# Second key stack of one stick-breaking head computed from its PSUM bank by ACT and DVE instead of two transfers from POOL's queue

## The chip, the cores and the metric

The kernel runs on one core of one Trainium2 chip. The metric is the device time of one execution in microseconds, given as the median of several runs. The engines are TensorE (PE, the matmuls), VectorE (DVE), ScalarE (ACT), GpSimd (POOL) and SyncE (SP); SP, ACT and POOL issue transfers on queues of their own. All data are float32.

## What is computed

The reference is two transformer blocks over 512 tokens of width 1024. The change lies in the first block's attention, which has four differential heads and eight stick-breaking heads of 64 dimensions. A stick-breaking head computes, in blocks of 128 queries:

```python
z = jnp.einsum('bhqd,bhkd->bhqk', q_blk, k).astype(jnp.float32) * scale
log_beta = jax.nn.log_sigmoid(z)
log_1mb = jnp.where(strict, jax.nn.log_sigmoid(-z), 0.0)
between = lax.cumsum(log_1mb, axis=3, reverse=True) - log_1mb
a = jnp.where(strict, jnp.exp(log_beta + between), 0.0)
return jnp.einsum('bhqk,bhkd->bhqd', a.astype(v.dtype), v)
```

A differential head takes two softmax maps p0 and p1 (with a position bias) and applies p0 - lam * p1 to its values; lam comes from four vectors of 64 numbers. The rest of the program is the projections, the gated feed-forward parts and the second block's mixer.

## The kernel before

Matmul operands are split into a rounded high part and the rest (`whi` by ACT's copy L107, `wlo` by a subtraction on DVE or POOL, L108), and a product is three matmuls (L128 to L130). A projection writes a PSUM bank; there are eight banks, and `PLAN_1` gives each kind of tile its banks by number.

Queries and keys come two heads to a bank, 64 partitions each. `stack_q` makes for each head one tile `qs` with the high part in 64 partitions and the rest in the other 64. `stack_k` makes `ka`, which holds the high part at the head's own partitions and the rest at the others, and `kb`, which is `ka` with its two halves exchanged. `ka` is computed from the bank: a copy on ACT (L417) and a subtraction on DVE (L418). `kb` is filled by two transfers from SBUF to SBUF on POOL's queue (L419 and L420), 64x512 numbers or 128 KB each. A score block is then two matmuls, `ka` by `qs` and `kb` by `qs` (L442), which add up all four products of the parts.

`start()` makes the stacks of the first pair of heads, S0 and S1, from banks 0 (`ps_mm_238`, queries) and 2 (`ps_s_239`, keys), and those of the second pair. Head `r` of a pair is the first (0) or the second (1). Then come, in the order of `PLAN_1`: the tables of the position bias (two gathers `rev` from the DRAM tile `scratch`, on POOL's queue, L382) and lambda (four loads into `lv`, L391 to L396), the first value projection v0 (banks `ps_mm_492` and `ps_mm_493`, `natural`), the heads S0 to S3, the second value projection v1 (`ps_mm_985` and `ps_mm_984`) and further projections, S4 to S7, and the differential heads D0 to D3.

A stick-breaking head has three units of scores, one bank each (S0: `ps_n_607`, `622`, `636`; S1: `700`, `715`, `729`). The steps of a unit: scores L442 and a mask L445; Abs, Exp and Ln on ACT (L448 to L450); maximum and sum on DVE (L451); the split `sph` and `spl` (L454 and L455); the cumulative sums on PE (L460 to L470); Exp on ACT into `a` (L476); the split `ah` and `al` (L481 and L482); the values on PE (L485 and L486). L678 and L679 add the two halves of its output `ot`. Value projections are evicted by L588 (ACT) and L589 (DVE). A differential head has scores L518, logits L508 (DVE), Exp L538 (ACT), lambda's factor L540 and L541, the difference of the maps on DVE (L547) or POOL (L544 and L545), transposes L568, evictions L121 and L122, and values L554.

The order on each engine is set by a scheduler at build time, with a cost model of its own, after the program has been recorded in `PLAN_1`'s order. So a change of one operation moves others.

Of the kernel before, what the change touches and what calls it, by code (L numbers as in the profile page):

```python
# [37 lines left out]
def f32(ap):  # L38
    return ap.bitcast(F32)
# [360 lines left out]
def stack_q(cx, q, r, pool, scale, t=None):  # L400

    nc = cx.nc
    a, b = slice(64 * r, 64 * r + 64), slice(64 - 64 * r, 128 - 64 * r)
    if t is None:
        t = pool.tile([P, T], F32R, tag="q", bufs=cx.nq, name="qs")
    nc.scalar.activation(t[a], q[a], AF.Copy, scale=scale)
    nc.vector.scalar_tensor_tensor(t[b], q[a], scale, f32(t[a]), op0=ALU.mult, op1=ALU.subtract)
    return t


def stack_k(cx, q, r, pool):

    nc = cx.nc
    a, b = slice(64 * r, 64 * r + 64), slice(64 - 64 * r, 128 - 64 * r)
    u = pool.tile([P, T], F32R, tag="k", bufs=cx.nk, name="ka")
    v = pool.tile([P, T], F32R, tag="k", bufs=cx.nk, name="kb")
    nc.scalar.copy(u[a], q[a])  # L417
    nc.vector.tensor_sub(u[b], q[a], f32(u[a]))  # L418
    nc.gpsimd.dma_start(v[0:64], u[64:128])  # L419
    nc.gpsimd.dma_start(v[64:128], u[0:64])  # L420
    return u, v
# [188 lines left out]
def attention_1(cx, I, first, finish):  # L610

    nc, tc = cx.nc, cx.tc
    w = I["w_qkv"][0]
    with tc.tile_pool(name="att1", bufs=1, reuse_waits="tile") as pool:
# [13 lines left out]
            mix[k] = m  # L628
        Q, K, v, o, z = {}, {}, {}, {}, {}

        def stacks(n, q, k):

            for out, st, bank in ((Q, lambda b, r: stack_q(cx, b, r, pool, 0.125), q), (K, lambda b, r: stack_k(cx, b, r, pool), k)):
                if bank is not None:
                    out.setdefault(n, []).extend(st(bank, r) for r in range(2))

        def start():

            first.append(cx.fetch(w, 0, KD, [(1536 + P, P)]))
            ww = [cx.split(st, lo_on=e) for st, e in zip(first, (nc.gpsimd, nc.gpsimd, None))]  # L640
            banks = [cx.bank(i) for i in ("mm", "s", "mm")]
            for c in (slice(0, 256), slice(256, T)):
                for q, wi in zip(banks, ww):
                    cx.columns_of(q, wi, c, c.start == 0)
            stacks("s0", banks[0], None)
            stacks("s0", None, banks[1])
            stacks("s1", banks[2], None)
            stacks("s1", None, cx.columns(cx.split(cx.fetch(w, 0, KD, [(2048 + P, P)]))))

# [44 lines left out]
        for x in PLAN_1:  # L694
            if isinstance(x, dict):
                cx.share(**x)
            elif x[0] == "+":
                cx.lo_on = nc.gpsimd if x[1] == "p" else nc.vector
            elif x == "start":
                start()  # L700
            elif x == "tables":
                z["band"], z["lam"] = diff_tables(cx, I, pool)
            elif x[0] == "b":
                z[x] = z["band"](int(x[1]))
            elif x[0] == "S":
                sb(int(x[1]))
            elif x[0] == "D":
                diff(int(x[1]))
            elif x[0] == "n":
                norm(x[1:])  # L710
            elif x[0] in "vw":
                value(x)
            else:
                project(x)
# [281 lines left out]
def mixer(cx, I, finish):  # L996
# [4 lines left out]
    with tc.tile_pool(name="mixer", bufs=1, reuse_waits="tile") as pool:  # L1001
# [15 lines left out]
        def keys(c0):  # L1017
            st = cx.fetch(w, 0, KD, [(c0, 128)])
            q = cx.columns(cx.split(st))
            return [stack_k(cx, q, g, pool) for g in range(2)]  # L1020
# [14 lines left out]
        for c in (slice(0, 256), slice(256, T)):  # L1035
            for q, wi in zip(banks, ww):
                cx.columns_of(q, wi, c, c.start == 0)
        KB = [stack_k(cx, banks[0], g, pool) for g in range(2)]
        QB = [stack_q(cx, banks[1 + h // 2], h % 2, pool, scale(h)) for h in range(4)]
        cx.share(mm=(0, 1), s=(2, 3), t=(4, 5), o=(6, 7))  # L1040
# [335 lines left out]
```

## Time and profile before

| | us |
|---|---|
| median of 3 runs | 1645.98 (1645.66 to 1646.47) |
| the profiled execution | 1645.26 |
| its span, first to last instruction | 1643.5 |
| outside the span | 1.76 |
| PE busy | 1613.6 (98% of the span) |
| DVE, ACT, POOL busy | 844.3, 680.3, 212.3 |
| mean granted clock of TensorE | 0.997 |

The profiled execution is one run of its own; it lies 0.72 us below the median. The span is what the trace covers, and the 1.76 us beside it are the start and the end of the program. Busy shares are means over the whole span; the first block's attention lies in the first 262 us or so of it. All waits below are read from that one execution.

### The profile page before, as it was taken

Reading aid. Unit: us, or ns where it says so; the run is one execution under the profiler, and the core shown is the slowest. Engines: PE = TensorE matmul, PEld = TensorE weight load, DVE = VectorE, ACT = ScalarE, POOL = GpSimd, SP = SyncE. Lnnn points to the kernel's source line nnn. Section 1 sums busy time; section 2 is a strip of 40 time slices with the busy share of each in tenths; the row PEclk is TensorE's granted clock in tenths of the full one; section 3 lists DMA queues with packets and bytes.
Section 4 is the critical chain, followed back from the end, with each engine's and each line's share of the span. In section 5 each row is a group of like instructions: output and inputs, shape, how many; then the busy total and the mean of one; then the engine's idle time right before and its main releaser. Section 6 shows DMA issues by size and latency. Waiting matters only on the chain.

```text
span 1643.5 us, 21090 instructions
## 1 busy us (share of the span) xinstructions
PE 1613.6 (98%) x8354; PEld 1375.0 (84%) x8354; DVE 844.3 (51%) x1391; ACT 680.3 (41%) x1212; POOL 212.3 (13%) x291
## 2 busy tenths in 40 slices
PE   8999999999999999999999999999999999999998
PEld 7988987888888888888888888888878988888886
DVE  5667776666665235433333225687985533333232
ACT  4656565444444123323232223576874432222222
POOL 3044241000000001000000000034770000000000
PEclk9999999999999999999999999999999999999999
DMA  6434315433223234333332325462005532232231
GB/s 187 111 104 114 91 40 188 147 103 103 94 86 103 90 102 154 128 103 102 103 103 92 101 90 162 115 168 65 15 27 183 188 103 96 84 101 104 90 103 64
DMA packets 149451, 177.02 MB, mean 108 GB/s; under 512 B 5999, under 2 KB 116031, under 8 KB 149352
## 3 DMA queue, kind: packets, MB, share of 16 engines
q1 hardware_dynamic: 141798, 158.35, 29.9%
q0 software_dynamic: 4672, 7.87, 2.1%
q10 hardware_dynamic: 2882, 9.44, 1.5%
q8 instruction: 66, 1.08, 0.3%
q14 instruction: 33, 0.27, 0.1%
HBM read 159.37 MB, written 10.51 MB: 103 GB/s over the span
## 4 chain that ended last, share of the span: by engine, by line
PE 91%; DVE 3%; DMA 2%; ACT 2%; POOL 1%; issue 1%; SPq 0%; POOLq 0%; DVEq 0%; ACTq 0%
PE ps_mm L128 11%; PE ps_mm L129 11%; PE ps_mm L130 11%; PE ps_n L130 9%; PE ps_n L129 9%; PE ps_n L128 9%; PE ps_s L130 8%; PE ps_s L128 8%; PE ps_s L129 8%; PE ps_s L518 1%; PE ps_t L568 1%; PE ps_o L1086 1%; PE ps_o L1087 1%; PE ps_n L194 1%; DMA kb<-ka 1%
## 5 line engine op out<-in xcount | busy, mean ns | idle before, releaser
L108 DVE TENSOR_TENSOR wlo<-stage,whi 128x1024 fp32r<-128x1024 f32 (+1 forms) x242 | 297.7, 1232 | 462.8 <-ACT whi L107 459.1
L107 ACT CAST whi<-stage 128x1024 fp32r<-128x1024 f32 x256 | 268.2, 1050 | 604.1 <-PE ps_mm L129 200.6
L128 PE MATMUL ps_mm<-HT,whi 128*128 128x512 f32 (+1 forms) x824 | 306.7, 372 | 3.3 <-ACT HT L196 2.1
L129 PE MATMUL ps_mm<-HT,whi 128*128 128x512 f32 (+1 forms) x824 | 306.2, 372 | 0.5 <-DVE HT L197 0.2
L130 PE MATMUL ps_mm<-HT,wlo 128*128 128x512 f32 (+1 forms) x824 | 305.3, 371 | 0.0
L130 PE MATMUL ps_s<-HT,wlo 128*128 128x512 f32 (+1 forms) x560 | 209.9, 375 | 2.0 <-DVE wlo L108 2.0
L128 PE MATMUL ps_s<-HT,whi 128*128 128x512 f32 (+1 forms) x560 | 209.9, 375 | 0.0
L129 PE MATMUL ps_s<-HT,whi 128*128 128x512 f32 (+1 forms) x560 | 209.6, 374 | 0.0
L129 PE MATMUL ps_n<-wlo,gh 128*128 128x512 f32 x480 | 186.8, 389 | 0.0
L130 PE MATMUL ps_n<-whi,gl 128*128 128x512 f32 x480 | 186.7, 389 | 0.0
L128 PE MATMUL ps_n<-whi,gh 128*128 128x512 f32 x480 | 186.7, 389 | 0.0
L128 PEld LDWEIGHTS ps_mm<-HT,whi 128*128 128x128 f32 x824 | 156.5, 190 | 29.6 <-ACT HT L196 4.2
L129 PEld LDWEIGHTS ps_mm<-HT,whi 128*128 128x128 f32 x824 | 156.2, 190 | 26.4 <-DVE HT L197 1.5
L130 PEld LDWEIGHTS ps_mm<-HT,wlo 128*128 128x128 f32 x824 | 156.2, 190 | 25.6 <-DVE wlo L108 0.3
L130 PEld LDWEIGHTS ps_s<-HT,wlo 128*128 128x128 f32 x560 | 105.8, 189 | 20.8 <-DVE wlo L108 2.2
L129 PEld LDWEIGHTS ps_s<-HT,whi 128*128 128x128 f32 x560 | 105.9, 189 | 18.9
L128 PEld LDWEIGHTS ps_s<-HT,whi 128*128 128x128 f32 x560 | 105.8, 189 | 18.5
L128 PEld LDWEIGHTS ps_n<-whi,gh 128*128 128x128 f32 x480 | 90.1, 188 | 18.9
L129 PEld LDWEIGHTS ps_n<-wlo,gh 128*128 128x128 f32 x480 | 90.1, 188 | 18.8
L130 PEld LDWEIGHTS ps_n<-whi,gl 128*128 128x128 f32 x480 | 90.1, 188 | 18.3
L225 POOL TENSOR_TENSOR r<-ms,mh 128x1 f32<-128x1 f32 x12 | 7.1, 590 | 730.9 <-DVE ms L224 728.2
L797 DVE TENSOR_TENSOR silu<-silu,ps_s 128x512 f32<-128x512 f32 x44 | 30.3, 688 | 137.2 <-PE ps_s L130 135.8
(333 smaller groups left out, 2481.0 us busy)
## 6 DMA issues: line engine op xcount, KB each, us to landing
stage<-in_ffn_w_in_dram SPq DMA_DIRECT2D x40, 1024.0 KB, 5.0
stage<-in_w_up_dram SPq DMA_DIRECT2D x20, 1024.0 KB, 5.0
stage<-in_ffn_w_out_dram SPq DMA_DIRECT2D x20, 1024.0 KB, 5.0
stage<-in_w_down_dram SPq DMA_DIRECT2D x10, 1024.0 KB, 4.9
stage<-in_w_qkv_dram SPq DMA_DIRECT2D x16, 512.0 KB, 5.0
xd<-x ACTq DMA_DIRECT2D x16, 512.0 KB, 2.6
x<-xd SPq DMA_DIRECT2D x16, 512.0 KB, 5.1
stage<-in_w_mix_out_dram SPq DMA_DIRECT2D x6, 1024.0 KB, 5.0
```

The source lines that it names most:

```text
L107: self.nc.scalar.copy(hi, src)
L108: (lo_on or self.lo_on).tensor_sub(lo, src, f32(hi))
L128: mm(out, a[0], b[0], start=first, stop=False, **kw)
L129: mm(out, a[0], b[1], start=False, stop=False, **kw)
L130: mm(out, a[1], b[0], start=False, stop=last, **kw)
L194: nc.tensor.transpose(q[:, k, :], h[:, (u * 4 + k) * P:(u * 4 + k + 1) * P], self.ident)
L225: nc.gpsimd.tensor_tensor(r, ms, self.minus_half[:, :1], op=ALU.pow)
L518: cx.nc.tensor.matmul(q[i], Q[:, t * P:(t + 1) * P], kk[:, 0:(t + 1) * P], start=t != 1 and s == 0, stop=s == 1, skip_group_check=True)
L568: cx.nc.tensor.transpose(q[:, n:n + P], p[r][:, j * P:(j + 1) * P], cx.ident)
L797: nc.vector.tensor_mul(a, a, up)
L1086: mm(o, v.rearrange("k x d -> k (x d)"), p[0], start=first, stop=False, skip_group_check=True)
L1087: mm(o[:64], v[:, 0], p[1], start=False, stop=False, skip_group_check=True)
```

## The change

`stack_k` gets a flag `direct`. With it, `kb` is computed from the head's PSUM bank like `ka`: its high part by a copy on ACT into the other 64 partitions, and the rest by a subtraction on DVE, and the two transfers are not issued. `start()` sets it for the second head of the first pair (S1) alone. The lines behind it move by 1 and later by 5, so L442 of before is L447 of after, L589 is L594, L508 is L513, L554 is L559 and so on.

```diff
-def stack_k(cx, q, r, pool):
+def stack_k(cx, q, r, pool, direct=False):
+
 
     nc = cx.nc
     a, b = slice(64 * r, 64 * r + 64), slice(64 - 64 * r, 128 - 64 * r)
@@
     v = pool.tile([P, T], F32R, tag="k", bufs=cx.nk, name="kb")
     nc.scalar.copy(u[a], q[a])
     nc.vector.tensor_sub(u[b], q[a], f32(u[a]))
+    if direct:
+        nc.scalar.copy(v[b], q[a])
+        nc.vector.tensor_sub(v[a], q[a], f32(u[a]))
+        return u, v
     nc.gpsimd.dma_start(v[0:64], u[64:128])
     nc.gpsimd.dma_start(v[64:128], u[0:64])
     return u, v
@@
-        def stacks(n, q, k):
-
-            for out, st, bank in (..., (K, lambda b, r: stack_k(cx, b, r, pool), k)):
+        def stacks(n, q, k, direct=()):
+
+            for out, st, bank in (..., (K, lambda b, r: stack_k(cx, b, r, pool, r in direct), k)):
@@
-            stacks("s0", None, banks[1])
+            stacks("s0", None, banks[1], (1,))
```

The scheduler's order differs between the two programs from the key stacks on through the first block's attention, and is the same behind it. On PE the first scores and the first value projection change places. Before, S0's scores are complete before v0 (`ps_mm_492`, `ps_mm_493`), and S1's unit 0 stands between its two halves of 48 matmuls:

```order
L442 MATMUL ps_n_607<-qs_385,kb_392 128x128
L445 MATMUL ps_n_607<-squares_r_454 128x2x128
L128 MATMUL ps_mm_492<-whi_494,HT_64 128x256
L129 MATMUL ps_mm_492<-wlo_495,HT_64 128x256
...
L130 MATMUL ps_mm_492<-whi_546,HT_64 128x256
L442 MATMUL ps_n_700<-qs_388,ka_397 128x256
L442 MATMUL ps_n_700<-qs_388,kb_398 128x256
...
L445 MATMUL ps_n_700<-squares_r_454 128x2x128
L128 MATMUL ps_mm_493<-whi_494,HT_64 128x256
```

After, S0's unit 2 (`ps_n_636`) is followed by the first `ka` matmul of each of S1's units and by v0, and behind all 96 matmuls of v0 come S0's unit 0, the rest of S1's scores and the first matmul of v1:

```order
L450 MATMUL ps_n_636<-squares_r_454 128x2x128
L447 MATMUL ps_n_700<-qs_388,ka_397 128x256
L447 MATMUL ps_n_715<-qs_388,ka_397 128x256
L447 MATMUL ps_n_729<-qs_388,ka_397 128x256
L128 MATMUL ps_mm_492<-whi_494,HT_64 128x256
...
L447 MATMUL ps_n_607<-qs_385,ka_391 128x256
...
L450 MATMUL ps_n_607<-squares_r_454 128x2x128
L447 MATMUL ps_n_700<-qs_388,kb_398 128x256
...
L128 MATMUL ps_mm_985<-whi_986,HT_64 128x256
```

S0's unit 0 (`ps_n_607`) has moved behind v0, and S1's `kb_398` is first used there.

On DVE, around lambda (`lv_477`, `ls_483`) and the first value evictions, before:

```order
L418 TENSOR_TENSOR ka_397<-ps_s_239,ka_397 64x512
L407 SCALAR_TENSOR_TENSOR qs_406<-ps_mm_240,qs_406 64x512
L391 TENSOR_TENSOR lv_477<-lv_477 128x2x64
L393 TENSOR_REDUCE ls_483<-lv_477 128x2
L395 TENSOR_TENSOR ls_483<-ls_483 128x1
L396 TENSOR_SCALAR ls_483<-ls_483 128x1
L108 TENSOR_TENSOR wlo_987<-stage_982,whi_986 128x1024
L418 TENSOR_TENSOR ka_440<-ps_mm_415,ka_440 64x512
L418 TENSOR_TENSOR ka_446<-ps_mm_415,ka_446 64x512
L451 SCALAR_TENSOR_TENSOR e_613<-ps_n_607,e_613 128x384
```

and after:

```order
L391 TENSOR_TENSOR lv_477<-lv_477 128x2x64
L422 TENSOR_TENSOR kb_398<-ps_s_239,ka_397 64x512
...
L108 TENSOR_TENSOR wlo_987<-stage_982,whi_986 128x1024
...
L419 TENSOR_TENSOR ka_440<-ps_mm_415,ka_440 64x512
...
L419 TENSOR_TENSOR ka_446<-ps_mm_415,ka_446 64x512
L108 TENSOR_TENSOR wlo_1039<-stage_982,whi_1038 128x1024
L594 TENSOR_TENSOR v_488<-ps_mm_492,v_488 128x4x64
L594 TENSOR_TENSOR v_489<-ps_mm_493,v_489 128x4x64
L108 TENSOR_TENSOR wlo_1102<-stage_1098,whi_1101 128x1024
L594 TENSOR_TENSOR v_488<-ps_mm_492,v_488 128x4x64
```

The new `L422` stands behind `L391`, and two weight splits (`wlo_1039`, `wlo_1102`) and four evictions have come ahead of S0's `e_613` (L451, L456 after).

On DVE, in the first differential heads, from the logits of D0's second map (`p_2234`) on to the first evictions, before, without the rows that only read out a minimum:

```order
L508 ISA p_2277,dst_2223<-ps_s_2279,band_1785 128x512
...
L108 TENSOR_TENSOR wlo_2832<-stage_2829,whi_2831 128x1024
L589 TENSOR_TENSOR v_2094<-ps_mm_2098,v_2093 128x256
L508 ISA p_2429,dst_2428<-ps_s_2430,band_1199 128x128
...
L122 TENSOR_TENSOR tl_2460<-ps_t_2455,th_2459 128x384
L407 SCALAR_TENSOR_TENSOR qs_2359<-ps_mm_2331,qs_2359 64x512
L508 ISA p_2481,dst_2428<-ps_s_2483,band_1199 128x384
```

and after:

```order
L108 TENSOR_TENSOR wlo_2832<-stage_2829,whi_2831 128x1024
L594 TENSOR_TENSOR v_2094<-ps_mm_2098,v_2093 128x256
L513 ISA p_2234,dst_2223<-ps_s_2235,band_1785 128x128
...
L513 ISA p_2470,dst_2428<-ps_s_2472,band_1199 128x512
L513 ISA p_2481,dst_2428<-ps_s_2483,band_1199 128x384
...
L513 ISA p_2482,dst_2428<-ps_s_2484,band_1199 128x512
...
L122 TENSOR_TENSOR tl_2460<-ps_t_2455,th_2459 128x384
```

`wlo_2832` and the last eviction of `v_2094` have moved ahead of the logits `p_2234`, and D1's last logits (`p_2481`, `p_2482`) ahead of `tl_2460`.

## Rows read from the trace of the kernel before

**Rows 1.** The page: busy time of each engine with its share of the span and its instructions, and the shares of the chain of work that ended last, by engine and by line.

```profile
PE 1613.6 (98%) x8354; PEld 1375.0 (84%) x8354; DVE 844.3 (51%) x1391; ACT 680.3 (41%) x1212; POOL 212.3 (13%) x291
...
PE 91%; DVE 3%; DMA 2%; ACT 2%; POOL 1%; issue 1%; SPq 0%; POOLq 0%; DVEq 0%; ACTq 0%
PE ps_mm L128 11%; PE ps_mm L129 11%; PE ps_mm L130 11%; PE ps_n L130 9%; PE ps_n L129 9%; PE ps_n L128 9%; PE ps_s L130 8%; PE ps_s L128 8%; PE ps_s L129 8%; PE ps_s L518 1%; PE ps_t L568 1%; PE ps_o L1086 1%; PE ps_o L1087 1%; PE ps_n L194 1%; DMA kb<-ka 1%
```

**Rows 2.** Waits of PE from 0 to 262 us: line and what it waited for, total us, times, longest.

```profile
PE ps_n L442 <- DMA kb<-ka: 2.0, 1, 2.0
...
PE ps_n L485 <- DVE ah L481: 1.1, 1, 1.1
PE ps_n L310 <- ACT ot L684: 0.7, 1, 0.7
...
PE ps_t L568 <- POOL p L545: 0.4, 1, 0.4
```

**Rows 3.** Timeline of PE around the wait (start, us, engine, line, operation, out<-in, shape; in brackets the idle time before it and what ended it).

```profile
48.69 0.28 PE L130 MATMUL ps_mm<-whi,HT 128*128 128x256 f32 x1
48.81 0.28 PE L442 MATMUL ps_n<-qs,ka 128*128 128x256 f32 x1
51.07 0.36 PE L442 MATMUL ps_n<-qs,kb 128*128 128x256 f32 x1 [1.98 <-DMA kb<-ka]
```

**Rows 4.** Three pieces of the chain (start us, us, what) and the issues of `kb` from 30 to 60 us (engine, number, KB each, median us from issue to landing).

```profile
36.79 4.06 DMA scratch<-vec
...
41.13 1.09 POOL rev L382 x2
42.22 8.72 DMA kb<-ka
...
kb<-ka POOLq DMA_DIRECT2D x8, 128.0 KB, 5.6
```

**Rows 5.** Timelines of DVE, POOL and PE around the wait at L485: the cast of `ah`, POOL's `wlo`, and the matmul that waited.

```profile
82.11 2.30 DVE L481 CAST ah<-a 128x384 fp32r<-128x384 f32 x1 [0.24 <-ACT a L476]
...
81.83 2.37 POOL L108 TENSOR_TENSOR wlo<-stage,whi 128x1024 fp32r<-128x1024 f32 x1 [32.35 <-ACT whi L107]
...
84.47 0.39 PE L485 MATMUL ps_n<-ah,v 128*128 128x256 f32 x1 [1.07 <-DVE ah L481]
```

**Rows 6.** Timelines of ACT and DVE around the key stacks of S0 and S1 and the lambda load.

```profile
37.06 0.58 ACT L417 CAST ka<-ps_s 64x512 fp32r<-64x512 f32 x1
38.64 0.59 ACT L406 ACTIVATE qs<-ps_mm 64x512 fp32r<-64x512 f32 x1 [1.00 <-DVE qs L407]
43.42 0.20 ACT L394 ACTIVATE ls<-ls 128x2 f32<-128x2 f32 x1 [4.18 <-DVE ls L393]
...
38.64 0.69 DVE L418 TENSOR_TENSOR ka<-ps_s,ka 64x512 fp32r<-64x512 f32 x1
...
42.77 0.29 DVE L391 TENSOR_TENSOR lv<-lv 128x128 f32<-128x128 f32 x1 [2.81 <-DMA lv<-in_lambda_k_dram]
```

**Rows 7.** Timelines of ACT and DVE where value evictions and weight splits stand one behind the other: starts give the pitch.

```profile
57.55 0.37 ACT L588 CAST v<-ps_mm 128x256 fp32r<-128x256 f32 x1 [1.83 <-PE ps_mm L130]
57.82 1.05 ACT L107 CAST whi<-stage 128x1024 fp32r<-128x1024 f32 x1
58.77 0.50 ACT L476 ACTIVATE a<-ps_n 128x384 f32<-128x384 f32 x1
59.15 0.38 ACT L588 CAST v<-ps_mm 128x256 fp32r<-128x256 f32 x1
...
51.60 0.42 DVE L589 TENSOR_TENSOR v<-ps_mm,v 128x256 fp32r<-128x256 f32 x1
51.93 0.68 DVE L455 TENSOR_TENSOR spl<-e,sph 128x512 fp32r<-128x512 f32 x1
...
58.91 1.23 DVE L108 TENSOR_TENSOR wlo<-stage,whi 128x1024 fp32r<-128x1024 f32 x1 [0.52 <-ACT whi L107]
60.05 0.35 DVE L481 CAST ah<-a 128x384 fp32r<-128x384 f32 x1
```

**Rows 8.** Timelines of ACT and DVE: the chain of one head from the first Abs (L448) to its first `spl` (L455).

```profile
73.00 1.37 ACT L448 ACTIVATE e<-ps_n 128x384 f32<-128x384 f32 x3
...
77.28 0.35 DVE L454 CAST sph<-e 128x384 fp32r<-128x384 f32 x1
...
78.02 0.55 DVE L455 TENSOR_TENSOR spl<-e,sph 128x384 fp32r<-128x384 f32 x1
```

**Rows 9.** Busy time in stretches around the first differential heads. Columns: the stretch, its length, the busy time of PE, PEld, DVE, ACT and POOL (instructions in brackets), the granted clock, the share of the DMA engines and their GB/s.

```profile
180.00:200.00 20.00, 20.00 (x156) 19.34 (x155) 13.79 (x35) 11.38 (x29) 5.28 (x7) 1.00 0.45 134
190.50:215.60 25.10, 25.10 (x155) 22.36 (x154) 19.21 (x52) 16.32 (x42) 8.71 (x12) 1.00 0.48 136
...
220.00:240.00 20.00, 19.61 (x120) 16.56 (x118) 17.55 (x59) 14.37 (x43) 12.17 (x12) 1.00 0.01 1
```

**Rows 10.** Timeline of PE, matmuls of 512 columns one behind the other; and of DVE, two logits of 384 and 512 columns.

```profile
85.14 0.40 PE L129 MATMUL ps_mm<-HT,whi 128*128 128x512 f32 x1
85.37 0.40 PE L130 MATMUL ps_mm<-HT,wlo 128*128 128x512 f32 x1
...
191.08 0.55 DVE L508 CUSTOM_DVE_ANT_0 p<-ps_s,band 128x384 f32<-128x384 f32 x1
...
191.56 0.69 DVE L508 CUSTOM_DVE_ANT_0 p<-ps_s,band 128x512 f32<-128x512 f32 x1
```

More of the change, by code (lines that the diff above doesn't have):

```diff
@@ L629, in attention_1 @@
         Q, K, v, o, z = {}, {}, {}, {}, {}
-        def stacks(n, q, k):
-            for out, st, bank in ((Q, lambda b, r: stack_q(cx, b, r, pool, 0.125), q), (K, lambda b, r: stack_k(cx, b, r, pool), k)):
+        def stacks(n, q, k, direct=()):
+            for out, st, bank in ((Q, lambda b, r: stack_q(cx, b, r, pool, 0.125), q), (K, lambda b, r: stack_k(cx, b, r, pool, r in direct), k)):
                 if bank is not None:
```

## The prediction

> **What bounds the kernel now.** I read the page first: TensorE (PE) is busy 98% of the span and the chain of work that ended last is PE for 91% of it; "DMA kb<-ka" has 1% of the chain [rows 1], and the clock is granted in full [rows 9]. So time is won or lost only where PE stands still. The waits of PE over the first 262 us, the part of the program that the change re-orders, name these places [rows 2]: 2.0 us at the scores L442 for the second key stack `kb`, 1.1 at L485 for DVE's `ah`, 0.7 at L310, 0.4 at L568. The two near the end are bound by the tails of the differential heads, which keep their order.
>
> PE's timeline shows the 2.0 us: after 48 value matmuls the first score matmul with `ka` runs at 48.81 and the one with `kb` only at 51.07 [rows 3]. The chain says why: the half of `kb` issued at 42.22 took 8.72 us to land, against a median of 5.6 for the eight of this stretch [rows 4]. Ahead of it on POOL's queue stand two `rev` gathers, held until 41.13 by the transfer that writes `scratch`. The 1.07 us are another thing: POOL's `wlo` ran from 81.83 to 84.20, and a DVE cast of 128x384 that began at 82.11 took 2.30 us instead of 0.35, so PE waited until 84.47 [rows 5]; a cast of this size, alone, takes 0.35 [rows 8].
>
> **What goes.** The wait for `kb` goes: **-1.98**. That matmul now waits for a DVE subtraction which, as shown next, is done at 43.8, nine us ahead of its new place in PE's order. The wait at L485 goes too, since `wlo` and this cast no longer meet: **-1.07**, or nothing if they do. POOL loses two issues of 0.5 us, which nobody waited for; SP's list of loads is the same before and after.
>
> *The page on this.* "DMA: Bandwidth & Descriptors", section "Anatomy of one DMA — SWDGE (gpsimd) path", of the Trainium skill fits such a transfer as about 2.0 us plus bytes/436e3, an estimate of 2.3 us for 128 KB. By it the half would have landed at 44.5, nothing would have waited, and the sum would be 1.98 higher; the 8.72 measured decides, the queue being shared.
>
> **What is added.** One ACT copy of 64x512 (0.58 by L417) and one DVE subtraction (0.69 by L418) [rows 6]. The copy follows `qs` on ACT near 39.2, where ACT is idle until 43.42, so it costs nothing. The subtraction stands on DVE behind `lv`, which waits until 42.77 for the lambda load [rows 6]. It therefore runs at 43.1 to 43.8, and the PSUM bank of these keys, which S0's first unit wants next, is free 4 us later than the L418 at 38.64 left it. Queued behind it are the reduction of lambda and the `wlo` of the next weights; `whi` has been moved ahead of Exp (at 43.42 before), so its `wlo` can start at about 44.1, and PE has 96 matmuls of other weights ahead of it. Nothing is lost there.
>
> **What moves: the stick-breaking heads.** The late bank turns PE's order round. Before: S0's scores, 48 value matmuls, S1's unit 0, 48 more. After: two units of S0, the `ka` halves of S1, 96 value matmuls at a pitch of 0.12 us, then S0 unit 0 and the rest of S1, and at once the next value projection (`ps_mm_985`). That needs the first one's bank empty. PE gets there at 55.8 (48 x 0.12 = 5.8 after 48.8, plus some 1.2 of scores). The bank's last user is the second eviction of `v_488` by DVE (L589, L594 in the changed file). It is behind ACT's copy of `v_489` (its last matmul ends at 54.2; 0.3), `whi` (0.95 to the next start, 1.05 long) and DVE's `wlo` (1.15), all of it in a row [rows 7]: 54.5, 55.5, 56.7, and 0.4 for itself, 57.1. **+1.4** of PE, new.
>
> S1 follows with less filler in between. From the first Abs (L448) of a head's three units to the end of its first `spl` (L455) the trace shows 5.6 us (73.00 to 78.57) [rows 8]. Counted by pitch along the new order PE has 5.9 us of work from the end of S0's last unit to the use of `sph_711`, while `a` (0.4), that chain and a value eviction of 0.33 take 6.3 [rows 7], 6.6 with the 0.3 that a matmul lasts beyond its start: **+0.5**. Then DVE does in a row `sph_725`, L679, L589, `spl_726`, and PE, with 0.4 to 0.5 us of work between its uses, waits for `ot_606` (**+0.35**) and for `spl_726` (**+0.5**). Behind it `sph_740` is due when POOL's next `wlo` (2.4 us) has started: by the row at 82.11 a cast that meets it lasts until POOL is done. That would be +1.05; if the cast starts first, nothing. Laid out by these pitches POOL is ahead by 1 us, but its start hangs on a load and on ten ACT steps, so I take half: **+0.5**, with 0 and 1.05 in the range.
>
> *The page on this.* "SBUF — State Buffer", section "SBUF: two separate sides", of the Trainium skill says that a DVE operation in a two-port mode and a GpSimd one lock each other out for the whole instruction, so a meeting is paid in full or not at all. The 2.30 us agrees; by it this term is 1.05 or 0, and the sum 0.55 higher or 0.5 lower.
>
> Sum for S: +3.25, against 3.05 gone. Heads S2 to S7 come 5 to 17 us of PE work later than before, with their fillers in between: I count nothing, at most 1.
>
> **What moves: the first two differential heads.** S's delay has eaten filler, so D0 and D1 stand closer. From D0's second-map scores (`ps_s_2235`) to the use of `tl_2460` PE had, before, 25 us (190.5 to 215.6), and DVE was busy 19.2 of them [rows 9]. In the new order this piece of PE is 39 matmuls of 512 columns (39 x 0.23 = 9.0 [rows 10]), scores 4.2, transposes 0.8 and 2.0 of L554: 16.0 us. DVE's list for it loses two `wlo` (2 x 1.2) and two L589 (2 x 0.35), which are done ahead, and gains the last two logits of D1 (0.55 + 0.69 [rows 10]) and a `qs` (0.69, as L418): 19.2 - 3.1 + 1.9 = 18.0; added up row by row by start-to-start pitch it is 17.5, which I take. DVE cannot start before the four score matmuls are in, 0.5 us. So DVE's `tl_2460` is ready 18.0 us after PE's start, and PE waits 18.0 - 16.0 = **+2.0**, spread over several places. DVE's own idle time was 5.9 us of that stretch before; 2 us of it kept would make it +4. If half of the casts and `wlo` run ahead, it is +1. Behind it the orders agree again; the share of DVE there (17.55 of 20 at 220 to 240 [rows 9]) lets nothing be caught up.
>
> **The sum** against the profiled execution: 1645.26 - 1.98 - 1.07 + 3.25 + 2.0 = 1647.46. The median of the runs shown lies 0.72 above that execution, so +2.2 on the median gives **1648.2 us**.
>
> **The rivals.**
> 1. *Clean gain.* The new waits stay hidden and the stage loses only its own. For it: all waits of 41 to 262 us together are 4.3 us, so a gain is at most that; 2.0 to 3.0 is the natural size: 1643.0 to 1644.0, and 1641.7 at the bound. Against it: the bank `ps_mm_985` waits for is behind five steps in a row.
> 2. *Exchange.* One wait takes the place of another: the value bank costs 1.4, S1 0.9, DVE in D0/D1 keeps up by running ahead: -3.05 + 2.3 to 3.3, 1645.2 to 1646.2. For it: before, DVE was idle 6 of 20 us from 180 to 200 [rows 9].
> 3. *DVE becomes the bound in D0/D1* and idles there as before: +4, the cast met +1.05, S2 to S7 +0.5: -3.05 + 3.8 + 4 + 0.5 = +5.2, 1651.2. It decides (over 0.2%) from +3.1 in D on.
> 4. *The transfer was hidden anyway* is excluded: PE names it, 1.98 idle. That the direct copy isn't used is excluded by the order, where the two new instructions stand.
>
> **Chances.** Measurement tells a change of 0.2%, 3.3 us. Forecast case (+0.6 to +4.0) 0.45; clean gain 0.15, a third of it beyond 0.2%; exchange 0.18; DVE-bound 0.22. Of the forecast case a quarter lies over +3.3: slower 0.22 + 0.11 = 0.33, faster 0.05, same 0.62. The range leaves out the outer end of the clean gain and what lies over case 3: 1644.0 to 1651.2; the forecast's own is 1646.6 to 1650.0.
>
> **What the changed profile would show.** No PE wait for `kb` near 50 and "L442" rows for S1 in one run behind 96 value matmuls. A PE wait of about 1.4 at the first value matmul after them, released by DVE `v`. Waits of 0.3 to 1 at 70 to 78 on `spl`, `ot` and `sph`, with or without a cast of over 2 us. PE idle of some 2 us in small pieces around 200 to 222, released by DVE and ACT. From about 245 on both traces run alike. I am wrong if PE's idle time between 41 and 262 falls below 4.3 us, or if the largest new wait lies on a line not named here.

## The result: slower by half a per cent, and the profile after

The changed kernel takes **1654.65 us** (median of 6 runs, 1652.15 to 1660.35) against 1645.90 beside it: 1.0053 times the time before, 95% interval 1.0043 to 1.0064. That is +8.7 us where +2.2 was forecast, and 3.5 above the upper end of the range. The profiled execution took 1657.87, 3.2 above this median (before: 1645.26, 0.7 below its own).

The page of the changed kernel, the two lines that answer to [rows 1]:

```profile
PE 1620.8 (98%) x8354; PEld 1380.0 (83%) x8354; DVE 851.0 (51%) x1392; ACT 681.0 (41%) x1213; POOL 210.7 (13%) x289
...
PE 89%; DVE 4%; DMA 2%; ACT 2%; issue 1%; POOL 1%; SPq 0%; POOLq 0%; ACTq 0%; DVEq 0%
```

PE has the same 8354 matmuls and is busy 7.2 us longer with them. Waiting itself doesn't count as busy, so most of this must be matmuls that ran slower: the mean granted clock of this execution is 0.994, against 0.997 before. In the chain, PE's share falls from 91 to 89% and DVE's rises from 3 to 4%.

The waits of PE from 0 to 280 us, which answer to [rows 2] (line and what it waited for, total us, times, longest):

```profile
PE ps_mm L128 <- DVE v L594: 2.6, 3, 1.2
PE ps_n L465 <- DVE spl L460: 2.5, 2, 2.3
...
PE ps_t L573 <- POOL p L550: 1.4, 1, 1.4
PE ps_s L523 <- DVE dst L513: 1.0, 1, 1.0
```

The waits for `kb` and for `ah` of [rows 2] are gone, as forecast. In their place stand waits for `v`, `spl`, `dst` and `p`. Their places on PE (timeline; in brackets the idle time ahead):

```profile
59.35 0.36 PE L128 MATMUL ps_mm<-whi,HT 128*128 128x256 f32 x1 [1.23 <-DVE v L594]
76.35 0.44 PE L465 MATMUL ps_n<-spl,squares_r 128*128 128x384 f32 x1 [0.26 <-DVE spl L460]
80.38 0.80 PE L465 MATMUL ps_n<-spl,squares_r 128*128 128x512 f32 x1 [2.27 <-DVE spl L460]
...
197.24 0.36 PE L128 MATMUL ps_mm<-whi,HT 128*128 128x256 f32 x1 [1.00 <-DVE v L594]
...
223.27 0.44 PE L523 MATMUL ps_s<-ka,qs 128*128 128x384 f32 x1 [1.01 <-DVE dst L513]
225.52 1.21 PE L573 MATMUL ps_t<-ident,p 128*128 128x128 f32 x7 [1.36 <-POOL p L550]
```

The wait of 2.27 us from 78 on has its cause in two rows, one of POOL and one of DVE:

```profile
77.41 2.38 POOL L108 TENSOR_TENSOR wlo<-stage,whi 128x1024 fp32r<-128x1024 f32 x1 [27.90 <-ACT whi L107]
...
77.48 2.85 DVE L460 TENSOR_TENSOR spl<-e,sph 128x512 fp32r<-128x512 f32 x1
```

It is the meeting of [rows 5] again, in another place: a subtraction that takes 0.68 elsewhere [rows 7] began 0.07 us behind POOL's `wlo` and ended 0.5 us behind its end. What the changed kernel does to the clock is seen in the busy times by stretch (columns as in [rows 9]; the granted clock is the number behind POOL's):

```profile
76.00:78.00 2.00, 1.71 (x10) 1.23 (x9) 2.00 (x5) 2.00 (x5) 0.59 (x1) 1.00 0.03 8
78.00:80.00 2.00, 0.12 (x1) 0.00 (x0) 2.00 (x1) 0.20 (x1) 1.79 (x1) 0.91 0.00 0
80.00:82.00 2.00, 1.62 (x5) 1.43 (x6) 2.00 (x6) 0.00 (x0) 0.00 (x0) 0.50 0.00 0
82.00:84.00 2.00, 2.00 (x7) 1.69 (x6) 0.56 (x1) 0.00 (x0) 0.00 (x0) 0.50 0.00 0
84.00:86.00 2.00, 2.00 (x6) 1.54 (x5) 0.00 (x0) 0.00 (x0) 0.00 (x0) 0.50 0.00 0
86.00:88.00 2.00, 2.00 (x9) 1.60 (x9) 0.00 (x0) 0.00 (x0) 0.00 (x0) 0.88 0.00 0
88.00:90.00 2.00, 2.00 (x15) 1.79 (x13) 0.00 (x0) 0.58 (x2) 0.00 (x0) 1.00 0.00 0
...
226.00:228.00 2.00, 2.00 (x11) 1.66 (x9) 1.80 (x7) 1.90 (x5) 0.15 (x1) 0.61 0.00 0
228.00:230.00 2.00, 2.00 (x13) 2.00 (x11) 1.99 (x9) 1.86 (x8) 0.00 (x0) 0.54 0.00 0
```

From the wait at 78 on the granted clock falls to 0.50, the lower level of 1.2 GHz. PE is busy there, but its matmuls of 512 columns, 0.23 us apart in [rows 10], come 0.43 apart:

```profile
84.07 0.63 PE L129 MATMUL ps_mm<-HT,whi 128*128 128x512 f32 x1
84.50 0.63 PE L130 MATMUL ps_mm<-HT,wlo 128*128 128x512 f32 x1
```

The clock falls again behind the two waits at 222 to 225. In [rows 9] it was 1.00. The kernel before has such a stretch too, but far behind the first attention (0.50 from 1112 to 1116 us).

To say where the 12.6 us between the two spans (1643.5 and 1656.1) lie, I compare starts of PE's matmuls. Two parts hold the same matmuls in every order: the *first part*, from the start of the 186th matmul (36.6 us before the change) to that of the 1,159th (189.4), which holds the stick-breaking heads, and the *second part*, up to the 1,521st (249.5), with D0 and D1; a wait ahead of the 1,159th is counted with the second. For the two kernels and the eleven runs of the next section (us; "idle" by PE's rows):

| kernel (described below) | first part | idle in it | second part | idle in it | median of its runs |
|---|---|---|---|---|---|
| before | 152.79 | 3.06 | 60.07 | 1.21 | 1645.9 |
| after | 157.25 | 4.12 | 66.06 | 4.42 | 1654.65 |
| x1, direct copy, old order | 150.57 | 1.08 | 60.05 | 1.23 | 1641.27 |
| x1b, the same again | 150.56 | 1.08 | 60.05 | 1.18 | 1641.86 |
| x2, transfers, new order | 156.98 | 4.11 | 66.16 | 4.63 | 1657.44 |
| x3, new order, POOL's `wlo` later | 152.25 | 1.94 | 65.98 | 5.22 | 1651.14 |
| x4, x1 with that `wlo` on DVE | 149.08 | 0.02 | 60.07 | 1.20 | 1642.06 |
| r0, before in its own order, written out | 154.89 | 3.67 | 60.07 | 1.23 | 1646.41 |
| x5, transfer ahead of the gathers | 151.30 | 1.57 | 60.05 | 1.19 | 1643.31 |
| x6, new order in the first part | 157.40 | 4.12 | 64.50 | 4.04 | 1652.06 |
| x7, new order in the second part | 150.69 | 1.08 | 67.10 | 6.22 | 1652.03 |
| x8, copy's subtraction late | 154.04 | 2.85 | 60.07 | 1.22 | 1645.77 |
| x9, later still | 156.12 | 4.93 | 60.06 | 1.23 | 1648.50 |

So the change costs 4.46 us in the first part and 5.99 in the second; 1.7 more of the profiled execution lie ahead of the 186th matmul, where PE's waits add up to 6.9 against 5.7 us, and 0.4 behind the 1,521st. Both differ from run to run.

### The profile page after: what moved, and what is told of

The parts are those of the page before. It is cut to its first block, busy times and chain, and to the rows that moved or that the text cites. A ratio compares the mean times of both kernels' runs of the same rounds, so it can differ in the third digit from the quotient of the medians.

```text
span 1656.1 us, 21078 instructions
## 1 busy us (share of the span) xinstructions
PE 1620.8 (98%) x8354; PEld 1380.0 (83%) x8354; DVE 851.0 (51%) x1392; ACT 681.0 (41%) x1213; POOL 210.7 (13%) x289
## 3 DMA queue, kind: packets, MB, share of 16 engines
q8 instruction: 66, 1.08, 0.3%
## 4 chain that ended last, share of the span: by engine, by line
PE 89%; DVE 4%; DMA 2%; ACT 2%; issue 1%; POOL 1%; SPq 0%; POOLq 0%; ACTq 0%; DVEq 0%
PE ps_mm L128 11%; PE ps_mm L129 11%; PE ps_mm L130 11%; PE ps_n L128 9%; PE ps_n L130 8%; PE ps_n L129 8%; PE ps_s L130 8%; PE ps_s L128 8%; PE ps_s L129 8%; PE ps_s L523 1%; PE ps_t L573 1%; DVE wlo L108 1%; PE ps_o L1091 1%; PE ps_o L1092 1%; DMA stage<-in_cmp_v_w_dram 1%
```

## The experiments

All eleven programs below have their order written out: for each engine a list of instruction numbers, and between neighbours of a list an edge that fixes the order and waits for nothing.

```python
for line in table.strip().splitlines():          # one line per engine
    ...
    tc.add_manual_dep(traced[name], prev, mybir.DependencyInfo(
        mybir.DependencyClass.NoSync, mybir.DependencyReason.DATA), reason="ordered")
```

With it the copy and the order, which the scheduler changes together, can be had one without the other. Diffs of lists are given by the instructions' outputs and lines.

**Does the written form cost anything?** (r0)

> The kernel before, its own order on every engine written out as a list of instruction numbers (the form in which the orders of the other experiments are given). If the written form costs and gains nothing, 1646.3 (1645.5 to 1647.0) and the same waits, the 2.0 us at the S1 key stack among them. If the form itself gives some 3 us, 1643, and then 3 of the 5 us that the changed program won in the old order are the form's and not the copy's.

Measured: 1646.41 (11 runs) against 1646.18 beside it, ratio 1.0001 [0.9993, 1.001]. The form costs and gains nothing.

**The copy without the new order** (x1, and again x1b).

```diff
 ACT    qs_406 (L406)
+ACT    kb_398 copy (L421)
 ACT    ls_483 (L394)
 DVE    qs_406 (L407)
+DVE    kb_398 subtraction (L422)
 DVE    lv_477 (L391)
-POOL   kb_398 transfer
-POOL   kb_398 transfer
```

> The changed kernel, with the issue order of every engine written out so that it is that of the kernel before; the two new instructions stand behind `qs_406` on ACT and on DVE, ahead of lambda. Theory A (the order costs, the copy does not): the 1.98 us wait for `kb` is gone and the rest as before, 1645.9 - 2.0 = 1643.9 us, between 1643.2 and 1644.8; granted clock 1.00 from 41 to 262 us. Theory B (the two instructions themselves or the later bank cost, in any order): new waits behind ACT or DVE, 1648 or more.

> The changed program in the order of before once more, as the base of the two runs beside it: 1641.3 (1640.5 to 1643.6), no wait for the S1 key stack, granted clock 1.00 from 41 to 256 us.

Measured: 1641.27 (6 runs; 0.997 [0.9958, 0.9982]) and 1641.86 (7 runs; 0.9971 [0.996, 0.9982]). Waits of PE from 38 to 262 us, second run:

```profile
PE ps_n L490 <- DVE ah L486: 1.1, 1, 1.1
PE ps_n L310 <- ACT ot L689: 0.7, 1, 0.7
PE ps_t L573 <- POOL p L550: 0.3, 1, 0.3
```

The wait for `kb` is gone and nothing came in its place. The copy by itself is worth 5 us, more than the 2 that the profile before had shown; the last experiment takes this up. This version is faster than both kernels, and none of the others is faster than it.

**The new order without the copy** (x2).

```diff
-ACT    kb_398 copy (L421)
-DVE    kb_398 subtraction (L422)
+POOL   kb_398 transfer   (behind the same neighbours on POOL as before)
+POOL   kb_398 transfer
```

> The kernel before, with both transfers for `kb`, in the issue order that the changed kernel has (the transfers behind the same neighbours on POOL as before). Theory A: as slow as the changed kernel, 1652 to 1658 us, with the long wait for `spl` near 80 us and the granted clock at half of its full rate behind it; no wait for `kb`, which lands near 51 and is wanted at 54. Theory B: no slower than before, 1644 to 1647.

Measured: 1657.44 (5 runs), 1.0062 [1.005, 1.0075]. Waits of PE, 38 to 262 us:

```profile
PE ps_mm L128 <- DVE v L589: 2.6, 3, 1.2
PE ps_n L460 <- DVE spl L455: 2.5, 2, 2.3
```

No wait for `kb` here, and the four largest waits are those of the changed kernel to a tenth: in this order PE comes to `kb` so late that the transfer was hidden anyway. All of the loss is the order's.

**POOL's `wlo` out of the subtraction's way** (x3): in the new order, the ACT step that POOL's `wlo` waits for goes two places down.

```diff
 ACT    v_981 (L593)
-ACT    whi_1306 (L107)
 ACT    v_980 (L593)
 ACT    a_760 (L481)
 ACT    v_981 (L593)
+ACT    whi_1306 (L107)
```

> The changed kernel in its own order, with one ACT instruction (`whi_1306`, L107) issued two places later, so that POOL's `wlo_1307` starts near 79 in place of 77.4 us and misses the DVE subtraction `spl_726`. Theory A1 (the wait of 2.27 us is this meeting, and the low clock behind it follows from the wait): wait under 0.7, granted clock 1.00 from 78 to 88, 1654.65 - 1.7 - 3.9 = 1649 us. Theory A2 (the clock falls there anyway, by the thin work of this order): 1653, clock still below 0.9 from 78 to 88.

Measured: 1651.14 (7 runs), 1.0027 [1.0017, 1.0038]. The wait for `spl`, POOL's `wlo` and what it meets now, and the stretches around 80 us:

```profile
PE ps_n L465 <- DVE spl L460: 0.3, 1, 0.3
...
78.05 2.77 POOL L108 TENSOR_TENSOR wlo<-stage,whi 128x1024 fp32r<-128x1024 f32 x1 [29.54 <-ACT whi L107]
...
78.48 2.56 DVE L486 CAST ah<-a 128x384 fp32r<-128x384 f32 x1
```

```profile
76.00:80.00 4.00, 3.89 (x20) 3.04 (x20) 4.00 (x8) 1.81 (x3) 1.95 (x1) 1.00 0.02 4
80.00:84.00 4.00, 4.00 (x24) 3.44 (x22) 1.59 (x2) 0.58 (x2) 0.82 (x1) 1.00 0.00 0
84.00:88.00 4.00, 4.00 (x21) 3.28 (x19) 2.46 (x5) 4.00 (x10) 0.87 (x1) 1.00 0.00 0
```

`wlo` still meets DVE, but now the cast of `ah`, 2.56 us long, for which PE doesn't wait. With the subtraction out of the way the 2.27 us go and the clock stays at 1.00: the first part falls from 157.25 to 152.25, 5.0 us for one meeting, of which 2.2 is idle time and 2.8 the slower matmuls behind it. By the medians it is 3.5. The second part keeps its cost, with the clock at 1.00 all through.

**The other meeting** (x4): x1 with that `wlo` on DVE, so that the one of [rows 5] goes too.

```diff
-            stacks(n, cx.columns(cx.split(st[:, :, :P])), None)
+            stacks(n, cx.columns(cx.split(st[:, :, :P], lo_on=nc.vector if n == "s3" else None)), None)
```

> As x1, and the first weight rest of the last stick-breaking projection (`wlo_1307`) computed by DVE behind `al_858` in place of POOL, so that no POOL instruction runs beside the cast of `ah_857`. If that meeting alone made the 1.07 us wait at L485: x1 less 1.0, 1642.9 us. If DVE is then late for the matmuls that use `wlo_1307`: no gain, 1643.9 or up to 1.0 more.

Measured: 1642.06 (8 runs), 0.9974 [0.9964, 0.9985]. On DVE the cast and the moved `wlo` stand one behind the other:

```profile
81.56 0.36 DVE L486 CAST ah<-a 128x384 fp32r<-128x384 f32 x1 [0.24 <-ACT a L481]
82.63 1.22 DVE L108 TENSOR_TENSOR wlo<-stage,whi 128x1024 fp32r<-128x1024 f32 x1
```

The cast is back at 0.36, PE's wait at L490 is gone, and the first part is 1.5 us shorter than in x1. The median isn't: 1642.06 lies within the runs of x1 and x1b (1640.08 to 1643.58). That the meeting makes the wait is shown; that the gain reaches the whole time is not.

**Which part of the order costs** (x6 and x7): the changed program with the new order up to the boundary at about 187 us and the old one behind it, and the other way round.

```diff
 order of every engine, x6:
-after, after
+after up to the 1,158th matmul, before's from there on
 order of every engine, x7:
-after, after
+before's up to the 1,158th matmul, after from there on
```

> The changed program; up to about 187 us (the S heads) every engine goes by the order of the changed kernel, behind that (D0 and D1) by the order of before. If the two parts cost apart from each other, the S part alone costs 1.2 (value bank) + 2.3 and 0.3 (subtraction beside POOL) + 3.9 (half clock) less 1.1 (the wait at L490 that the new order avoids) = +6.6 over the 1641.3 of the old order, less about 0.7 of slack, 1647.2 (1645.5 to 1648.5). If the waits in D0 and D1 only come from the lateness of the S part, all of it stays: 1653 to 1655.

> The mirror image: the changed program in the order of before up to about 187 us and in that of the changed kernel behind it. If the order within D0 and D1 is what costs there, the waits at L128 for v (1.0), at L523 for dst (1.0) and at L573 for p (1.4) come back, PE idles some 5 us between 187 and 256 us instead of 1.2, with or without a short fall of the clock at about 225 us: 1641.3 + 4 to 6.5, 1646.6 (1645 to 1648). If they come from the S part being late, none comes back and the time is 1641 to 1642.

Measured: x6 1652.06 (5 runs; 1.004 [1.0028, 1.0053]), x7 1652.03 (11 runs; 1.0034 [1.0023, 1.0044]). x6's time decides nothing by itself, since the seam brought a wait that neither kernel has:

```profile
PE ps_n L322 <- DVE nat L318: 2.9, 1, 2.9
```

with a granted clock of 0.67 behind it. Read by parts it is clear: its first part takes 157.40 like the changed kernel's, 6.8 over x1, and its second 64.50, which is 60.05 and the seam (2.9 idle, the rest slow matmuls). No wait for `v`, `dst` or `p` follows in the second part, so these don't come from the heads being late. x7 shows where they do come from:

```profile
PE ps_mm L128 <- DVE v L594: 1.6, 1, 1.6
PE ps_s L523 <- DVE dst L513: 1.4, 2, 1.0
PE ps_t L573 <- POOL p L550: 1.4, 1, 1.4
PE ps_n L490 <- DVE ah L486: 1.1, 1, 1.1
```

They are all back, behind a first part of 150.69: the order within D0 and D1 makes them. The second part costs 7.0 over x1 (67.10), with the clock at 1.00 in this execution. The time is 5.4 above what I expected; the eleven runs reach from 1648.0, at a mean granted clock of 0.999, to 1654.5 at 0.995, so in a part of them the clock was lower as well; where in the program, no trace shows.

**Where the wait for `kb` came from** (x5).

```diff
 POOL   kb_398 transfer
+POOL   kb_398 transfer
 POOL   rev_1201 gather
 POOL   rev_1204 gather
-POOL   kb_398 transfer
```

> The kernel before, one DMA moved: on POOL's queue the second transfer of the S1 key stack stands ahead of the two reversed gathers instead of behind them; nothing else moves. If the 2.0 us wait came from what stood ahead of it in the queue, the wait shrinks below 0.5 us and the time is 1644.3 to 1644.8, so that most of what the direct copy wins could be had without it. If the transfer's own landing time made the wait, the wait stays at 1.5 to 2 us and the time at 1646.

Measured: 1643.31 (11 runs), 0.9986 [0.9977, 0.9995], 2.9 below before. From the chain, and PE's waits:

```profile
39.64 9.82 DMA kb<-ka
```

```profile
PE ps_n L442 <- DMA kb<-ka: 0.5, 1, 0.5
```

Both theories hold a piece. The issue comes 2.58 us sooner than in [rows 4] (39.64 for 42.22), but the transfer takes 9.82 instead of 8.72 and lands only 1.5 us sooner. Going ahead of the gathers takes away three quarters of the wait. The slow landing is as much a condition of it: at the median of 5.6 [rows 4] the half issued at 42.22 would have landed at 47.8, ahead of its use.

**What a wait costs when the clock answers** (x8 and x9): x1 with the copy's subtraction further down on DVE, so that PE must wait for it. (What PE waits for is not `kb`, which it uses only behind 48 value matmuls: the matmul in the rows below is the first of S0's unit 0, which goes into the bank that the subtraction reads.)

```diff
-DVE    kb_398 subtraction (L422)
 DVE    lv_477, ls_483, ls_483, ls_483 (L391 to L396)
+DVE    kb_398 subtraction (L422)      x8
 DVE    wlo_987 (L108)
+DVE    kb_398 subtraction (L422)      x9, in place of the line above
```

> The changed program in the order of before, one DVE instruction moved: the subtraction that finishes the S1 key stack stands behind the four small lambda steps (start 40.3 before, about 43.8 now), so that PE waits for it some 2.5 us at about 42 us; nothing else moves. Theory that a wait costs itself alone: 2.5 + 0.2 over the base, 1644.0, clock 1.00 behind the wait. Theory that a wait of this size also lets the granted clock fall for some microseconds (as in the changed kernel at 80 us, and in the repeated kernel of before at 50 us): 1645.5 to 1647.5 and a granted clock below 1.00 between 44 and 60 us.

> As the late subtraction, but behind one more DVE instruction (the 1.23 us weight subtraction that starts at 44.4): PE waits some 4.4 us. Wait alone: 4.6 over the base, 1645.9. With the clock: 1647.5 to 1649.5, clock below 1.00 behind the wait, and for longer than behind the shorter wait if the length of the wait sets the length of the fall.

Measured: x8 1645.77 (10 runs), x9 1648.50 (10 runs), 3.9 and 6.6 over x1b. PE's timeline and the stretches behind the wait, of x8:

```profile
44.63 0.36 PE L447 MATMUL ps_n<-qs,ka 128*128 128x256 f32 x1 [1.77 <-DVE kb L422]
```

```profile
46.00:48.00 2.00, 2.00 (x11) 2.00 (x11) 0.46 (x1) 1.98 (x5) 0.51 (x1) 0.50 0.75 178
48.00:50.00 2.00, 2.00 (x15) 2.00 (x13) 1.32 (x3) 1.98 (x5) 1.02 (x2) 0.70 0.41 81
```

and of x9:

```profile
48.40 0.36 PE L447 MATMUL ps_n<-qs,ka 128*128 128x256 f32 x1 [3.85 <-DVE kb L422]
```

```profile
48.00:50.00 2.00, 1.60 (x10) 1.64 (x11) 0.93 (x2) 0.75 (x2) 0.51 (x1) 0.79 0.59 130
50.00:52.00 2.00, 2.00 (x11) 2.00 (x11) 0.00 (x0) 1.98 (x5) 0.00 (x0) 0.50 0.32 66
52.00:54.00 2.00, 2.00 (x16) 2.00 (x16) 1.56 (x3) 1.98 (x5) 1.02 (x2) 0.85 0.26 53
```

Both waits came out 0.5 to 0.7 shorter than expected, and behind both the clock fell. Against x1b the first part grew by 3.48 for 1.77 idle, and by 5.56 for 3.85 idle: 1.7 beyond the wait each time. A wait twice as long costs its own length more, and no more in clock. The rows say where the 1.7 comes from: what the granted clock lacks to 1.00, times the 2 us of each row, adds up to 1.6 in x8 and 1.7 in x9. (In the changed kernel, from 78 to 88 us, it is 3.4, of which a part falls into the wait itself.) The same is seen in r0, whose PE waited 2.59 us for `kb`:

```profile
50.00:52.00 2.00, 0.21 (x2) 0.01 (x1) 2.00 (x5) 1.13 (x3) 0.40 (x1) 1.00 1.00 162
52.00:54.00 2.00, 1.20 (x10) 1.23 (x11) 2.00 (x6) 0.38 (x1) 0.00 (x0) 1.00 0.06 17
54.00:56.00 2.00, 2.00 (x13) 2.00 (x13) 0.61 (x2) 0.00 (x0) 0.00 (x0) 0.59 0.00 0
56.00:58.00 2.00, 2.00 (x12) 2.00 (x12) 0.00 (x0) 0.14 (x1) 0.00 (x0) 0.55 0.00 0
```

Its first part took 4.3 us longer than x1b's, for 2.6 of idle time. So the order of before pays for `kb` either 2.2 us, as in the profile that I had, or 4.3, as here; and the 5 us that x1 wins by the medians are nearer to the second, and above both. How often each happens I can't say from two traces, and what makes the rest of the 5 us stays open. Mean clocks of the whole runs point the same way: 0.996 to 0.998 in most runs of before, 0.998 to 0.999 in all thirteen of x1 and x1b.

## Why the prediction was wrong, point by point

The new waits came in the two places that the prediction named, the heads up to S1 and D0/D1; what failed is their price. The sum fell 8.5 us short: D0 and D1 were put 4.0 too low, the clock, 2.8, at nothing, and the remaining 1.7 lie in waits of the first part that were longer than forecast (0.9 of idle time) or dearer than their rows.

- **The waits that go** were right. `kb`: -1.98 forecast, and x1 against before gives -2.22 in the first part. `ah`: -1.07, gone in the changed kernel. The subtraction was forecast for 43.1 to 43.8 and ran at 44.44, 1.3 us late with the lambda load; nothing waited for it.
- **The value bank** was right: +1.4 forecast behind "five steps in a row", 1.23 found, at the named matmul, released by the named instruction.
- **S1** had the right chain and the wrong victim. The first `spl` cost 0.26 instead of 0.5, and PE never waited for `ot_606`. The step that failed here is that "`sph_740` is due when POOL's next `wlo` (2.4 us) has started": POOL came one DVE instruction sooner and met `spl_726`. I had 0.5 for that subtraction and 0.5 for a possible meeting; together they cost 2.27. "SBUF — State Buffer", section "SBUF: two separate sides", of the Trainium skill names this case: a DVE operation with two SBUF inputs is locked out too while GpSimd reads SBUF. The 2.85 us of the row at 77.48 agrees. I had applied it to casts alone, and weighed a 1 us uncertainty in POOL's start over a single instruction instead of over all that stand there.
- **D0 and D1** were mis-sized, and this is the step with the largest error, 4.0 of the 8.5 us by which the sum fell short: +2.0 forecast, +6.0 found (66.06 against 60.07), and 5.9 with the clock at 1.00 (x3). I summed DVE's work over the whole stretch and set the end against the end. The waits stand in the middle: 1.00 for `v`, then 1.01 for `dst` and 1.36 for POOL's `p`, which the sum didn't hold at all. Each time PE has waited, later slack can't pay for it. Rival 3 had this as +4, the nearest of the cases.
- **The clock** was put at nothing without a reason, and this is the second step that failed: [rows 9] showed 1.00, and I carried that over to an order with longer waits. In the first part the meeting's fall is 2.8 us by x3. In the second, the clock fell too (0.61 and 0.54 at 226 to 230), but the part is as long as in x3, where it didn't: while PE ran slower, DVE caught up, and waits of 0.46 and 0.29 that x3 has are missing. By the medians, x1 to x2 or after, the order costs 13 to 16 us.
- **A wait is dearer than its row.** From x1b to before, one wait of 1.98 added 2.23 with no fall of the clock. [rows 3] show how: the matmul with `kb` would have started 0.12 behind the one at 48.81 and started at 51.07, which is 2.14 lost, and it then lasted 0.36 for the 0.28 of its neighbours. The idle time of a row is counted from the modelled end of the matmul ahead, and that end overlaps the start of a successor that doesn't wait. From x1b to x3, idle time in the second part grew by 4.0 us and the part by 5.9 with the clock at 1.00: five more waits, 1.9 us beyond their rows. The forecast counted waits by their idle time alone.
- **The sum again**, by measured pieces against x1b: the new order's first part +6.7 (157.25), its second +6.0 (66.06), together +12.7. 1641.9 + 12.7 is 1654.6, and the median is 1654.65. That it fits so well is luck in part, since the pieces come from one execution that lies 3.2 above this median; the pieces of x2 give 1654.4 in the same way, for a median of 1657.44. The forecast had +2.2 and +2.0 there (without `kb`), so 8.5 short.
- **"Wrong if the largest new wait lies on a line not named here"**: it lay on `spl`, a tile named there for a wait of 0.3 to 1, by a mechanism named for its neighbour. PE's idle time in the two parts grew from 4.3 to 8.5 us, so the other sign didn't come up either: neither asks what a wait costs beyond its idle time. **Rival 4**, excluded, was right in an odd way: in the new order the transfer is hidden (x2), so the copy brings nothing there.

What stays open: why the scheduler's order of D0 and D1 differs so much for a bank freed 4 us later, and which of its moves makes each of the three waits; x7 shows only that it is the order of that part.

## What to carry to other kernels

When an edit lets a scheduler reorder a stage, the edit and the order are two changes: take the edit alone, in the old order, before judging it (here -5 us and +13). Check what every long GpSimd instruction can meet on VectorE, subtractions with two SBUF inputs as well as casts, and move the start to where it meets one that TensorE doesn't wait for (x3). Where TensorE is nearly full, price a new wait of about 2 us at about twice its length (3.5 for 1.77, 4.3 for 2.59, 5.0 for 2.27 here), until the granted clock behind it has been read.

## What the runs showed of the hardware that I had not expected

- The granted clock fell to 0.50 (1.2 GHz) behind PE waits of 1.77, 2.27, 2.59 and 3.85 us, and of 1.01 and 1.36 close together; it stayed at 1.00 behind 1.98 (before), 1.23 (after), and behind the same pair of 1.01 and 1.35 in x3. The length of the wait alone doesn't decide it, and I found nothing else in the rows that does.
- Behind one and the same wait the clock falls in one execution and not in the next. All thirteen traces have a wait of 1.93 to 1.96 us for a `wlo` behind the reordered part (at 288.5 before, 300.7 after), and the clock fell behind it in eight of the traces and stayed at 1.00 in five. So a single trace that shows no fall, as x3 near 80 us, doesn't prove that there is never one; x3's medians bear it out with 3.5 us. Before, and after:

```profile
288.00:292.00 4.00, 3.46 (x29) 3.46 (x30) 3.40 (x7) 0.00 (x0) 1.07 (x2) 1.00 0.62 201
...
300.00:304.00 4.00, 3.27 (x18) 3.27 (x19) 3.40 (x7) 0.00 (x0) 1.06 (x2) 0.69 0.58 190
```

- At one place the price of a fall doesn't go with the wait: 1.7 us beyond the idle time behind 1.77 and behind 3.85 alike. At another, where the clock stayed at 0.50 for longer (80 to 86 us), it was 2.8.
- A transfer issued 2.58 us sooner landed 1.5 us sooner: 9.82 us for 8.72.
